# Keys and the first query pair of a windowed-attention trunk, seven block products for eight

## Chip, cores and metric

The kernel runs on one core of one Trainium2 chip. The metric is the device time of one execution in microseconds. Before the change three runs gave 1925.84, 1926.04 and 1926.89 us, so the median is 1926.04 us.

## What is computed

The reference is a trunk of two layers over 1024 tokens of width 1024, in float32. Layer 0 mixes tokens by a short gated convolution, layer 1 by attention in a window of 128 tokens; a SwiGLU of width 2816 follows each. Only the attention layer matters here:

```python
def swa_sink_attention(h, w_qkv, q_gain, k_gain, sinks, w_o):
    qkv = h @ w_qkv                       # 16 query heads, 4 key and 4 value heads of 64
    ...
    q = rmsnorm(q, q_gain)                # per head
    k = rmsnorm(k, k_gain)
    ...
    scores = jnp.einsum('bnqkgd,bnskd->bnkgqs', qb, kw).astype(jnp.float32) * scale
    ...                                   # ALiBi, window mask, a sink column, softmax
    out = jnp.einsum('bnkgqs,bnskd->bnqkgd', p.astype(vw.dtype), vw)
    return out.reshape(bsz, s, N_Q_HEADS * HEAD_DIM) @ w_o
```

## The kernel before

Everything lies transposed: features on the 128 partitions, the 1024 tokens along the free dimension, so the normed input `xs` is eight tiles of 128 features. To keep float32 accuracy every operand is split in a rounded part and a rest, and every block of a product is three matmuls of 128x512: rounded by rounded, rounded by rest, rest by rounded. A plain product of 128 output columns over all tokens is 8 x 3 x 2 = 48 such matmuls (`product`, L177).

Most products of the kernel are made another way, for a pair of 128 columns at once: the operands are cut in 2 x 2 blocks, and seven products of sums of blocks take the place of eight products of blocks. Each of the seven is four blocks of features deep and covers half of the tokens, 12 matmuls; a pair is 7 x 12 = 84 instead of 2 x 48 = 96. The weights of one of the seven are a granule of 128x512, loaded, rounded by one engine and its rest taken by another (`split_granule`). Products 0, 1 and 6 read blocks of `xs` itself; products 5, 2, 3 and 4 read sums of blocks (`operand_sums`, L1714), which are made once, stored to `q_ops` in HBM and loaded back for each pair. The sums of weight blocks are made beforehand by DMAs with addition (`added_sums`, L889, into `q_sums`).

The order of the work is written by hand. A `Line` (L842) holds TensorE work end to end, at 0.2265 us a matmul by its own count, and other instructions hung on it at times of that count; whatever stands earlier on the line is issued earlier, and each engine works through its instructions in that order. `attention_layer` (L1658) hangs keys and values on the line of layer 0 (`keys_and_values`, L1810): two plain products for the two key tiles, the values, one plain product for query tile 0. For a key tile `key_stats` (L1894) makes sums of squares by 16 matmuls of two columns, then on VectorE and ScalarE a mean, a logarithm, an exponential, a Newton step and a spread to 128x512; `key_rows` (L1920) transposes that spread, scales the keys, and writes the split keys `kz` (`part`: a ScalarE and a VectorE copy and two VectorE subtractions for each half of the heads). `keep_v` (L1771) brings the values out of PSUM.

After the line come steps (`step`, L2229). A step holds, in the order of the letters of `ORDER`, up to one unit of attention (the scores of one head tile and one block of 128 queries, the stages of earlier units) and three pieces of filling matmuls, five or six in all; `plan` and `agenda` put other instructions into steps. The scores of all units are written to one PSUM bank, `P0`, which `maxima` (L2079) on VectorE empties. `LAG` is the number of steps before the first unit. Before the change the filling is query tile 1 by a plain product (8 steps), then the query pairs 1 to 3 by sevens (`query_pairs`, L2285). `keep_q` (L1981) norms a query tile as keys are normed; its rests are taken on GpSimd (`part_lo`, L2029).

Of the kernel before, what the change touches and what calls it, by code (L numbers as in the profile page):

```python
# [15 lines left out]
P = 128  # L16
# [4 lines left out]
HD = 64  # L21
# [31 lines left out]
LAG = 12  # L53

QUERY_ORDER = (0, 5, 2, 6, 1, 3, 4)
STREAMED = (5, 2, 3, 4)
# [30 lines left out]
def trunk_kernel(ctx: ExitStack, tc: tile.TileContext, xT, small, w_in, w_out, w_qk, w_q, w_v, w_o, w_gu, w_dn, out):  # L87
# [746 lines left out]
    q_sums = tc.dram_tile((4, GROUP, P, 5 * P), F32, name="s4")  # L834
# [229 lines left out]
    def channel_mixer(layer, next_stage, src_of, operands, raw_tags, extra_tags, keep_tags, slots, begin_with=(), first_w=None, line=None, lead_in=None, before=None, follow=None):  # L1064
# [450 lines left out]
        def down_product(u, k, granules):  # L1515
# [24 lines left out]
            def square():  # L1540
                if first or k == 6:
                    sq = slot(f"s{h}" if first else f"G{8 + u % 2}", (P, HALF))
                else:
                    sq = slot("WL", (P, HALF), bufs=2)
# [40 lines left out]
        if layer == 0:  # L1585
            first_added_sums(1, line, begin + 10.0, 18.0)
            for u, n in ((1, 1), (2, 2)):
                dst = [q_sums[i, u : u + n][:, :, 0 : 4 * P] for i in range(4)]
                parts = [w_q[e, u : u + n][:, :, r] for e in (0, 1) for r in (0, 1)]
                added_sums(dst, parts, line, steady_begins + 75.0 * u - 45.0, 9.0)  # L1590
# [67 lines left out]
    def attention_layer():  # L1658
# [53 lines left out]
        v = []  # L1712

        def operand_sums(p, tags, t):  # L1714
# [6 lines left out]
            def first():  # L1721
                s["tiles"] = [slot(tag, (P, 2, 2, HALF), F32R) for tag in tags]
                s["t"] = [a[:, i] for a in s["tiles"] for i in (0, 1)]
                s["raw"] = [plain(x[:, 1]) for x in s["t"]]
                s["b12"] = plain(s["t"][3][:, 0])
# [17 lines left out]

            def store(i):
# [8 lines left out]
            for i in (0, 1):  # L1753
                at(t + 6.4, store, i)
# [55 lines left out]
        def keys_and_values():  # L1810
# [9 lines left out]
            def split(name, t, t_lo, hi_eng, lo_eng):  # L1820
                def hi():
                    w = it[name]
                    w.alloc()
                    act.copy(w.hi, w.raw) if hi_eng is act else hi_eng.tensor_copy(w.hi, w.raw)

                def lo():
                    w = it[name]
                    lo_eng.tensor_tensor(w.lo, w.raw, plain(w.hi), ALU.subtract)

                at(t, hi)  # L1830
                at(t_lo, lo)

# [765 lines left out]
```

## Time and profile before

| | |
|---|---|
| median of three runs | 1926.04 us |
| profiled execution, time and span | 1926.88 us, 1925.1 us |
| TensorE busy, share of the span | 1917.9 us, 100% |
| VectorE, ScalarE, GpSimd busy | 69%, 46%, 15% |
| mean granted clock of TensorE | 0.998 |

The profiled execution took 1.8 us beyond its span. In the profile PE is TensorE's matmuls, DVE is VectorE, ACT is ScalarE, POOL is GpSimd and SP the engine that issues most DMAs. A time behind a line (L170) is that of the kernel before. The ends of matmuls are modelled, so that neighbours overlap in the rows; the pace is read from one start to the next.

### The profile page before, as it was taken

To read this page: it belongs to the slowest core of one execution; us is meant where nothing else is said; L and a number is where in the kernel's file an instruction comes from. 1 tells how busy PE (TensorE), PEld (TensorE's weight loads), DVE (VectorE), ACT (ScalarE), POOL (GpSimd) and SP (SyncE) were. 2 spreads that over 40 slices of the span, in tenths; PEclk is the share of its full clock that TensorE was granted. 3 is DMA by queue.
4 is the path that set the end of the run, shared out by engine and by line. 5 is a ranking of instruction groups with operands and counts; after the bars stand their busy time and mean duration, and the time that the engine had idled before them with its cause. 6 is when DMAs were issued, how large, how long until landed. Compare 5 with 4: busy or idle time off the path is not lost.

```text
span 1925.1 us, 25387 instructions
## 1 busy us (share of the span) xinstructions
PE 1917.9 (100%) x9069; PEld 1604.1 (83%) x9069; DVE 1325.6 (69%) x2288; ACT 881.6 (46%) x1733; POOL 296.1 (15%) x382
## 2 busy tenths in 40 slices
PE   9999999999999999999999999999999999999999
PEld 8888888888888888888898888888888888888887
DVE  8997877975655666555775887788756665665543
ACT  5543464633333334544545787655233333344441
POOL 0011231011111100000023556310111111100000
PEclk9999999999999999999999999999999999999999
DMA  8897595377787638976255661142675575477562
GB/s 315 257 253 149 132 248 159 111 255 209 205 232 212 150 134 287 345 234 205 95 190 188 214 213 49 56 174 82 218 209 143 196 199 157 130 241 278 199 223 103
DMA packets 151262, 368.36 MB, mean 191 GB/s; under 512 B 15072, under 2 KB 26464, under 8 KB 151136
## 3 DMA queue, kind: packets, MB, share of 16 engines
q1 hardware_dynamic: 116864, 259.49, 39.5%
q0 software_dynamic: 34128, 107.23, 22.4%
q8 instruction: 71, 1.16, 0.2%
q14 instruction: 55, 0.45, 0.1%
q10 hardware_dynamic: 144, 0.03, 0.0%
HBM read 295.12 MB, written 145.23 MB: 229 GB/s over the span
## 4 chain that ended last, share of the span: by engine, by line
PE 96%; DVE 2%; ACT 1%; issue 1%; POOL 0%; POOLq 0%; DVEq 0%; ACTq 0%
PE acc L1002 16%; PE acc L1003 16%; PE acc L1005 16%; PE P L1002 10%; PE P L1003 10%; PE P L1005 10%; PE acc L170 4%; PE acc L2394 2%; PE acc L174 2%; PE P L2118 1%; PE acc L1132 1%; PE acc L1134 1%; PE acc L1133 1%; PE P L1676 1%; PE P L1793 1%; PE P L2075 1%
## 5 line engine op out<-in xcount | busy, mean ns | idle before, releaser
L1002 PE MATMUL acc<-XS,G 128*128 128x512 f32 x926 | 360.4, 389 | 0.0
L1003 PE MATMUL acc<-XS,G 128*128 128x512 f32 x926 | 360.2, 389 | 0.0
L1005 PE MATMUL acc<-XS,G 128*128 128x512 f32 x926 | 360.2, 389 | 0.0
L1002 PE MATMUL P<-A,G 128*128 128x512 f32 x550 | 214.1, 389 | 0.0
L1005 PE MATMUL P<-A,G 128*128 128x512 f32 x550 | 214.0, 389 | 0.0
L1003 PE MATMUL P<-A,G 128*128 128x512 f32 x550 | 214.0, 389 | 0.0
L1002 PEld LDWEIGHTS acc<-XS,G 128*128 128x128 f32 x926 | 173.8, 188 | 36.1
L1005 PEld LDWEIGHTS acc<-XS,G 128*128 128x128 f32 x926 | 173.8, 188 | 36.1
L1003 PEld LDWEIGHTS acc<-XS,G 128*128 128x128 f32 x926 | 173.8, 188 | 36.0
L1002 PE MATMUL acc<-A,G 128*128 128x512 f32 x442 | 172.1, 389 | 0.0
L1005 PE MATMUL acc<-A,G 128*128 128x512 f32 x442 | 172.0, 389 | 0.0
L1003 PE MATMUL acc<-A,G 128*128 128x512 f32 x442 | 171.9, 389 | 0.0
L936 DVE TENSOR_TENSOR G<-WL,G 128x512 fp32r<-128x512 f32 x168 | 115.1, 686 | 72.4 <-ACT G L935 72.4
L936 DVE TENSOR_TENSOR G<-WR,G 128x512 fp32r<-128x512 f32 (+1 forms) x216 | 144.4, 668 | 28.2 <-ACT G L935 28.2
L935 ACT CAST G<-WR 128x512 fp32r<-128x512 f32 (+1 forms) x216 | 130.5, 605 | 61.9 <-PE acc L1005 27.6
L935 ACT CAST G<-WH 128x512 fp32r<-128x512 f32 (+1 forms) x174 | 104.7, 602 | 84.3 <-PE acc L1005 41.1
L1334 ACT ACTIVATE G<-G 128x512 f32<-128x512 f32 x88 | 55.8, 634 | 159.6 <-DVE G L1431 152.4
L936 DVE TENSOR_TENSOR G<-WH,G 128x512 fp32r<-128x512 f32 (+1 forms) x174 | 115.7, 665 | 18.8 <-ACT G L935 18.7
L1005 PEld LDWEIGHTS P<-A,G 128*128 128x128 f32 x550 | 103.2, 188 | 21.4
L1003 PEld LDWEIGHTS P<-A,G 128*128 128x128 f32 x550 | 103.2, 188 | 21.4
L1002 PEld LDWEIGHTS P<-A,G 128*128 128x128 f32 x550 | 103.2, 188 | 21.4
L935 ACT CAST G<-WL 128x512 fp32r<-128x512 f32 x168 | 103.3, 615 | 24.5 <-DVE WL L884 12.9
(384 smaller groups left out, 3754.9 us busy)
## 6 DMA issues: line engine op xcount, KB each, us to landing
G<-h SPq DMA_DIRECT2D x70, 512.0 KB, 5.1
s<-in_w_dn SPq DMA_DIRECT2D x32, 704.0 KB, 7.7
h<-X POOLq DMA_DIRECT2D x44, 512.0 KB, 4.7
s<-s POOLq DMA_DIRECT2D x32, 704.0 KB, 7.3
WR<-s SPq DMA_DIRECT2D x74, 256.0 KB, 3.9
WR<-in_w_gu SPq DMA_DIRECT2D x36, 512.0 KB, 4.8
WH<-in_w_gu SPq DMA_DIRECT2D x36, 512.0 KB, 4.8
XS<-q_ops SPq DMA_DIRECT2D x36, 512.0 KB, 5.1
```

The costliest lines, as they stand in the source:

```text
L170: pe.matmul(ps.half(h), wh, xs[:, j, c], start=first and j == 0, stop=False)
L174: pe.matmul(ps.half(h), wl, xs[:, 0, c], start=False, stop=last)
L935: lambda: act.copy(out_hi, raw),
L936: lambda: lo_eng.tensor_tensor(out_lo, raw, plain(out_hi), ALU.subtract),
L1002: pe.matmul(ps, w[:, 0, c], x[:, 0, :], start=start and e == 0, stop=False, skip_group_check=True)
L1003: pe.matmul(ps, w[:, 0, c], x[:, 1, :], start=False, stop=False, skip_group_check=True)
L1005: pe.matmul(ps, w[:, 1, c], x[:, 0, :], start=False, stop=last, skip_group_check=True)
L1132: pe.matmul(ps, hi[:, kc], xs[:, 0, c], start=k == 0, stop=False, skip_group_check=True)
L1133: pe.matmul(ps, hi[:, kc], xs[:, 1, c], start=False, stop=False, skip_group_check=True)
L1134: pe.matmul(ps, lo[:, kc], xs[:, 0, c], start=False, stop=k == n_op - 1, skip_group_check=True)
L1334: state["silu"] = act.activation(x, x, AF.Silu)
L2394: pe.matmul(ps, g[:, w, c], x[:, b, :], start=begin and i == 0, stop=end and i == 2, skip_group_check=True)
```

## The change

The two key tiles become a pair of their own (`KEYS_AS_PAIR`) and query tiles 0 and 1 become pair 0; both go by sevens, on the line. The values are projected first. In these two pairs products 5, 2, 3 and 4 read the operand sums from the SBUF tiles in which they were made, and not from `q_ops`. The sums of squares of key tile 0 and 1 stand behind the sixth and the tenth of the 14 products, the transposes behind the 8th, 9th, 11th and 12th. The last of the values and of `kz` come in the first steps. `LAG` goes from 12 to 4. Operand sums use `G7` and `G4` for their raw sums and start earlier. Two more pairs of weights are summed by DMA, two weight tensors become one, and some tile names are swapped. The three pairs in the steps are as before.

```diff
-LAG = 12
+LAG = 4
...
+KEY_ORDER = (0, 1, 5, 2, 6, 3, 4)
+KEYS_AS_PAIR = 4
...
+                sq = slot(f"s{h}", (P, HALF)) if first else slot("WL", (P, HALF), bufs=2)
...
+            for i, (u, n) in enumerate(((0, 2), (2, 2), (KEYS_AS_PAIR, 1))):
+                dst = [q_sums[s, u : u + n][:, :, 0 : 4 * P] for s in range(4)]
                 parts = [w_q[e, u : u + n][:, :, r] for e in (0, 1) for r in (0, 1)]
...
+                if not workspace:
+                    rooms_ = [slot(tag) for tag in ("G7", "G4")]
+                    workspace.extend(a[:, h] for a in rooms_ for h in (lo_half, hi_half))
+                s["raw"] = [workspace[i] for i in (1, 2, 3, 0)]
+                s["b12"] = workspace[0]
...
-            load(("k", 0), w_qk[NK], NK, t - 12.0)
-            load(("k", 1), w_qk[NK + 1], NK, t - 9.0)
-            split(("k", 0), t - 5.5, t - 4.4, act, dve)
-            split(("k", 1), t + 2.2, t + 3.4, act, dve)
             for q in (0, 1):
-                load(("wv", q), w_v[:, 4 * q : 4 * q + 4, :], 4, t + (-2.5, 4.7)[q])
-                at(t + (7.0, 13.5)[q], split_v, q)
-                load(("q", q), w_qk[q], NK, t + 15.5 + q)
-                split(("q", q), t + (28.0, 44.0)[q], t + (29.0, 45.0)[q], dve, pool)
-            operand_sums(0, ("A2", "A3"), t - 1.0)
-            operand_sums(1, ("A0", "A1"), t + 5.5)
-            operand_sums(2, ("A4", "A5"), t + 13.0)
-            operand_sums(3, ("A2", "A3"), t + 19.5)
-            at(t + 16.0, score_buffers)
-
-            def project(name):
-                it[name, "acc"] = Acc()
-                yield from product(it[name, "acc"], it[name], xs)
-
-            def project_work(name):
-                steps = project(name)
-                for _ in range(3 * NK):
...
+            def part(g, e, i):
+                if g not in kz:
+                    kz[g] = pair_slot(f"A{g}"), pair_slot(f"A{g + 2}")
+                hi, lo = kz[g]
+                raw = key_raw[g]
+                rows, rest = (slice(x * HD, (x + 1) * HD) for x in (e, 1 - e))
+                if i == 0:
+                    act.copy(hi[rows, e, :], raw[rows, :])
+                elif i == 1:
+                    dve.tensor_copy(hi[rest, e, :], raw[rows, :])
+                else:
+                    to = rows if i == 2 else rest
+                    dve.tensor_tensor(lo[to, e, :], raw[rows, :], plain(hi[rows, e, :]), ALU.subtract)
...
+            project_values(0)
             line.work(4, mean)
             at(line.end + 0.05, token_rows)
-            project_keys(1)
-            key_stats(0)
-            project_values(0)
-            key_rows(0)
-            key_stats(1)
             project_values(1)
-            key_rows(1)
-            project_work(("q", 0))
+            operand_sums(3, ("G8", "G10", "G9", "G11"), line.end + 0.1)
+            first_pairs()
...
+        seq = [(KEYS_AS_PAIR, k) for k in KEY_ORDER] + [(u, k) for u in range(NK // 2) for k in QUERY_ORDER]
+        n_first = 2 * KINDS
...
+            rooms["raws"] = [x[:, i] for x in (wr, g0, g1) for i in (0, 1)]
+            rooms["grans"] = wl + [rooms["spare"], slot("G2", (P, 2, 4 * P), F32R)]
+            rooms["banks"] = [bank(f"P{i}") for i in range(3)]
...
+        def split_granule(j, hi_eng=dve, lo_eng=pool):
+            g, raw = gran_room(j), raw_room(j)
+            act.copy(g[:, 0], raw) if hi_eng is act else hi_eng.tensor_copy(g[:, 0], raw)
+            lo_eng.tensor_tensor(g[:, 1], raw, plain(g[:, 0]), ALU.subtract)
+
+        def bank_of(u, k):
+            four = rooms["banks"]
+            return four[2] if k in (4, 5, 6) else four[(u + 1) % 2 if k != 1 else u % 2]
...
+        def part_of_x(k, p):
+            return xs[2 * p + (k != 0)][:, :, halves_of[k == 6]]
...
+            def stats(g):
+                s["st", g] = bank("P3")
+                head_stats(s["st", g], s["side", g], 0, NB)
...
+            def wide(g, q):
+                spread(act, s["side", g][:, halves_of[q]], s["y", g][:, 4 * q : 4 * q + 4, :])
+
+            def rows(g, q):
+                s["rows"] = bank("P3")
+                turn_blocks(s["rows"], s["side", g][:, halves_of[q]])
+
+            def scale(g, q):
+                raw = key_raw[g][:, halves_of[q]]
+                dve.scalar_tensor_tensor(raw, raw, qkg, s["rows"], ALU.mult, ALU.mult)
...
+            def of_product(j, p):
+                u, k = seq[j]
+                x = summed[p][STREAMED.index(k)] if k in STREAMED else part_of_x(k, p)
+                all_of(three(j, p, x))
+
+            def stats_work(g):
+                line.work(4, stats, g)
+                t = line.end
+                at(t + 0.1, log, g)
+                at(t + 0.9, guess, g)
+                at(t + 1.6, newton, g)
+                for q in (0, 1):
+                    at(t + 2.4 + 0.6 * q, wide, g, q)
+
+            def rows_work(g, q):
+                line.work(2, rows, g, q)
+                at(line.end + 0.05, scale, g, q)
...
+            for j in range(n_first):
+                begins[j] = line.end
+                u, k = seq[j]
+                for p in range(NK // 2):
+                    line.work(3, of_product, j, p)
+                t = line.end
+                finish(u, k, lambda f, t=t: at(t + 0.05, f))
+                if j in (4, 6):
+                    g = 0 if j == 4 else 1
+                    for h in (0, 1):
+                        at(t + 0.8 + 0.65 * h, squares, g, h)
+                if j in (5, 9):
+                    stats_work(0 if j == 5 else 1)
+                if j in (7, 8, 10, 11):
+                    rows_work(j // 10, (j - 7) % 3)
+                if j == 9:
+                    for i in range(4):
+                        at(t + 0.1 + 0.5 * i, keep_v, 0, i)
+                    for e in (0, 1):
+                        for i, d in enumerate((2.1, 2.1, 3.3, 4.6)):
+                            at(t + d + 3.3 * e, it["part"], 0, e, i)
+                if j == 11:
+                    s["base"] = t
+            for j in range(n_first + 2):
+                if j < n_first:
+                    t = begins[j - 3] + 0.05 if j > 3 else begin + 14.0 + 2.4 * j
+                    at(t, split_granule, j, act, dve)
+                if j < 6:
+                    at(begin + 2.0 + 1.2 * j, load_granule, j)
+                else:
+                    at(begins[j - (6 if j < n_first else 4)] + 0.02, load_granule, j)
+            at(begins[n_first - 1] + 0.05, split_granule, n_first, act, dve)
+            for n in range(4):
+                at(begins[4] + 3.0 * n, load_operand, n)
+            at(begins[11] + 0.1, load_operand, 4)
+            at(begins[13] + 0.1, score_buffers)
+            pos["free"] = "P3"
...
+            def planned_from(d, f):
+                t = s["base"] + 1.3 * d
+                if t < line.end - 0.2:
+                    at(t, f)
+                else:
+                    agenda.setdefault(max(round((t - line.end) / 0.65) / 2, 0), []).append(f)
+
+            keep_q(0, lambda: raw_of_even(0), plan_=planned_from)
...
+                plan(0, lambda j=j: split_granule(j + 1, dve, dve if j < n_first + 2 else pool))
+                load_granule(j + 2)
...
-            keep_q(0, it[("q", 0), "acc"])
-            w = it["q", 1]
-            pairs = query_pairs()
-            for j in (0, 1):
-                pairs.load_granule(j)
-            pairs.load_operand(4)
-            for n in (5, 6):
-                pairs.load_operand(n)
-            acc = Acc()
-            work = product(acc, w, xs)
-            for k in range(NK):
-                step(work)
-                if k % 2:
-                    pairs.load_operand(k // 2)
-                if k == 5:
-                    pairs.split_granule(0)
-            run(work)
-            pairs.load_operand(7)
-            keep_q(1, acc, pairs.odd_raw)
...
+            rooms["banks"] = [bank("acc") for _ in range(4)]
+            pos["values"] = rooms["banks"][3]
+            for n in (5, 6, 7):
+                load_operand(n)
+            for i in range(4):
+                plan(0.5 * i, lambda i=i: keep_v(1, i))
+            for e in (0, 1):
+                for i, d in enumerate((1.0, 1.0, 2.0, 3.0)):
+                    plan(d + 2 * e, lambda e=e, i=i: it["part"](1, e, i))
+            keep_q(1, lambda: rooms["odd"], later=4)
```

## Rows read from the trace of the kernel before

**Rows 1.** The page: busy time of each engine; the chain that ended last.
```profile
PE 1917.9 (100%) x9069; PEld 1604.1 (83%) x9069; DVE 1325.6 (69%) x2288; ACT 881.6 (46%) x1733; POOL 296.1 (15%) x382
...
PE 96%; DVE 2%; ACT 1%; issue 1%; POOL 0%; POOLq 0%; DVEq 0%; ACTq 0%
```

**Rows 2.** PE's waits, whole span: us in total, times, longest.
```profile
PE P L2075 <- DVE mx L2090: 1.2, 3, 0.5
```

**Rows 3.** Windows: length, busy of PE, PEld, DVE, ACT, POOL, clock, DMA share, GB/s.
```profile
1014.00:1025.00 11.00, 11.00 (x61) 9.33 (x60) 2.08 (x8) 2.88 (x7) 1.17 (x2) 1.00 0.73 262
1025.00:1034.00 9.00, 9.00 (x52) 7.79 (x50) 4.49 (x7) 4.74 (x10) 5.73 (x4) 1.00 0.72 253
1034.00:1060.00 26.00, 26.00 (x161) 22.66 (x160) 20.01 (x66) 19.23 (x60) 11.68 (x10) 0.93 0.52 167
```

**Rows 4.** Timeline of PE: start, length, line, tiles, count, idle before.
```profile
951.05 1.07 PE L170 MATMUL acc<-XS,WH 128*128 128x512 f32 x4
...
961.93 1.84 PE L1884 MATMUL P<-cst,s 128*128 128x1 f32 x16
...
974.66 1.84 PE L1676 MATMUL acc<-cst,G 128*128 128x2 f32 x16
976.36 0.37 PE L1766 MATMUL acc<-G,XS 128*128 128x256 f32 x1
...
1023.03 0.60 PE L1793 MATMUL P<-cst,G 128*128 128x128 f32 x4
1023.39 0.70 PE L170 MATMUL acc<-XS,WH 128*128 128x512 f32 x2
...
1051.98 0.36 PE L2075 MATMUL P<-A,G 128*128 128x192 f32 x1
```

**Rows 5.** Timeline of ACT around the values and key tile 1.
```profile
983.81 0.47 ACT L1779 ACTIVATE A<-acc,r 128x256 fp32r<-128x256 f32 x1 [0.55 <-DVE A L1780]
...
990.93 0.22 ACT L1695 ACTIVATE hr_y<-hr_m 128x16 f32<-128x16 f32 x1 [1.26 <-DVE hr_m L1683]
...
992.86 1.14 ACT L1788 COPY G<-hr_y 128x512 f32<-128x512 f32 x2 [0.66 <-DVE hr_y L1709]
994.02 1.05 ACT L1942 CAST A<-G 64x1024 fp32r<-64x1024 f32 x1
```

**Rows 6.** Timeline of DVE, from the end of layer 0 into the steps.
```profile
951.25 0.69 DVE L1532 TENSOR_TENSOR X<-X,acc 128x512 f32<-128x512 f32 x1 [2.59 <-PE acc L1005]
...
983.29 0.48 DVE L1780 SCALAR_TENSOR_TENSOR A<-acc,r,A 128x256 fp32r<-128x256 f32 x1 [0.97 <-ACT A L1779]
...
992.65 0.18 DVE L1709 SCALAR_TENSOR_TENSOR hr_y<-hr_t,hr_y 128x16 f32<-128x16 f32 x1
...
995.20 0.69 DVE L1944 CAST A<-G 64x1024 fp32r<-64x1024 f32 x1
995.90 2.46 DVE L1947 TENSOR_TENSOR A<-G,A 64x1024 fp32r<-64x1024 f32 x2
...
1027.84 0.43 DVE L2338 CAST WL<-WR 128x512 fp32r<-128x512 f32 x1 [1.59 <-PE acc L174]
1028.30 1.66 DVE L2340 TENSOR_TENSOR WL<-WR,WL 128x512 fp32r<-128x512 f32 x1
...
1032.66 0.69 DVE L2340 TENSOR_TENSOR WL<-WR,WL 128x512 fp32r<-128x512 f32 x1
...
1051.04 0.48 DVE L2090 CUSTOM_DVE_ANT_0 s<-P,cst 128x192 f32<-128x192 f32 x1
```

**Rows 7.** Timeline of POOL: the rests of query tile 0.
```profile
1025.16 5.96 POOL L2032 TENSOR_TENSOR G<-G,G 64x512 fp32r<-64x512 f32 x4 [1.76 <-ACT G L2027]
```

**Rows 8.** Windows, PE alone: length, PE busy, clock, DMA share, GB/s.
```profile
1034.50:1035.00 0.50, 0.50 (x4) 0.76 0.87 336
...
1038.00:1038.50 0.50, 0.50 (x5) 0.83 0.93 254
```

**Rows 9.** DMA issues: tiles, queue, count, KB each, median us to landing.
```profile
WR<-s SPq DMA_DIRECT2D x74, 256.0 KB, 3.9
```

More of the change, by code (lines that the diff above doesn't have):

```diff
@@ new lines, in part_of_x, with three @@
+        def part_of_x(k, p):
+            return xs[2 * p + (k != 0)][:, :, halves_of[k == 6]]
+        def three(j, p, x):
+            u, k = seq[j]
+            ps, g = bank_of(u, k), gran_room(j)
+            c = slice(p * P, (p + 1) * P)
+            begin, end = k in (0, 1, 4, 5) and p == 0, p == NK // 2 - 1
+            for i, (w, b) in enumerate(((0, 0), (0, 1), (1, 0))):
+                pe.matmul(ps, g[:, w, c], x[:, b, :], start=begin and i == 0, stop=end and i == 2, skip_group_check=True)
+                yield
@@ new lines, in attention_layer, with room, load_operand @@
+        loads = [(k, p) for u, k in seq[n_first:] if k in STREAMED for p in range(NK // 2)]
+        first_rooms = {}
+        used = {"n": 0}
+        def room(n):
+            if n >= 5 and n < 8:
+                if n not in first_rooms:
+                    first_rooms[n] = slot(("G10", "G11", "G9")[n - 5], (P, 2, HALF), F32R)
+                return first_rooms[n]
+            r = n if n < 5 else (n - 8) % 5
+            return xs[2 * r][:, :, hi_half] if r < 4 else rooms["spare"]
+        def load_operand(n):
+            if n < len(loads):
+                k, p = loads[n]
+                src = q_ops[p, STREAMED.index(k)].rearrange("p (j c) -> p j c", c=HALF)
+                nc.sync.dma_start(plain(room(n)), src)
@@ new lines, in after_use, with work_of_pairs @@
+        def after_use(n):
+            if n < 5:
+                load_operand(n + 8)
+            elif n >= 8:
+                load_operand(n + 5)
+        def work_of_pairs():
+            n = 0
+            for j in range(n_first, len(seq)):
+                u, k = seq[j]
+                plan(0, lambda j=j: split_granule(j + 1, dve, dve if j < n_first + 2 else pool))
+                load_granule(j + 2)
+                for p in range(NK // 2):
+                    streamed = k in STREAMED
+                    x = room(used["n"]) if streamed else part_of_x(k, p)
+                    steps = three(j, p, x)
+                    for i in range(3):
+                        next(steps)
+                        n += 1
+                        if i == 2 and streamed:
+                            after_use(used["n"])
+                            used["n"] += 1
+                        if i == 2 and p == NK // 2 - 1:
+                            finish(u, k, soon)
+                            if k == 1:
+                                keep_q(2 * u, lambda u=u: raw_of_even(u))
+                            if k == 4:
+                                raw, side = raw_of_odd(u)
+                                keep_q(2 * u + 1, lambda raw=raw: raw, side, later=3 if u + 1 < NK // 2 else 2)
+                        if n % 7 in (2, 4, 5, 0):
+                            yield
```

348 lines of the change are left out of this document (121 added, 227 removed).

## Prediction

> **What bounds the kernel now.** The page comes first: TensorE is busy all of the span and 96% of the chain that ended last is TensorE's [rows 1]. So two things can move the time: how many matmuls there are, and whether TensorE has to wait. The waits of TensorE come next: in the steps it waits for VectorE three times, 1.2 us in all, each time for the maxima that empty the one bank of scores [rows 2]; between 951 us, where the attention layer begins, and 1075 us no wait of it is listed. The windows say what the other engines do there: in the 20 us ahead of the first scores VectorE works 2.08 + 4.49 = 6.6 us, and in the next 26 us, with attention, 20.0 us [rows 3]. So VectorE enters the steps rested and has some 6 us to spare in the first of them. The timeline of TensorE gives the prices: 48 matmuls of 128x512 from 951.05 to 961.93, 0.2267 us each; a burst of 16 matmuls of two columns from 974.66 to 976.36, 1.70 us, where the line counts 4 x 0.2265 = 0.91; four transposes from 1023.03 to 1023.39, 0.36 us [rows 4]. A thing to see there is how close VectorE already is: the maxima of a unit start at 1051.04 and take two instructions of 0.48 us, and the next unit's scores start at 1051.98, just behind them [rows 4, 6].
>
> **The matmuls.** Two pairs of 96 matmuls become two of 84. 24 x 0.2267 = 5.44 us less. Bursts, transposes and values stay in number. This term is certain.
>
> **The first wait: key tile 1.** Take the end of product 10 as zero. TensorE does the burst for key tile 1 (1.70) and product 11 (12 x 0.2267 = 2.72), and at 4.42 it comes to the transposes of the spread of key tile 1, which are work of the line itself: all 3 products left stand behind them. Between burst and spread lie one VectorE mean, a logarithm, an exponential, three small VectorE instructions and a ScalarE spread. By themselves they would take 0.2 + 0.22 + 0.22 + 3 x 0.18 + 0.57, under 2 us [rows 5, 6], ready at 3.7. But the change hangs the values of the first half and key tile 0 on the line at the same place, and they are issued ahead. ScalarE has, in order: the copy of product 10's bank (0.57 as the spread's half), two values (0.47 each), a granule (0.57), the logarithm, two values, the exponential, a part of key tile 0 (1.05) and then the spread: from 0.2 to 5.3 without a single pause. And it pauses: the second value of a bank waits until VectorE has read the first, 0.55 us in the row at 983.81 [rows 5], and VectorE has its own queue: value rests 0.48 each, the granule's rest 0.69, a cast of key tile 0 of 0.69, all ahead of steps of the chain [rows 6]. Going down both queues:
>
> ScalarE bank copy to 0.8, value to 1.2; VectorE rest to 1.7; ScalarE value to 2.2, VectorE rest to 2.7; ScalarE granule to 2.8, VectorE its rest to 3.5; mean 3.6, logarithm 3.9; ScalarE value to 4.2, VectorE rest to 4.8, value to 5.3, exponential to 5.4; VectorE rest and cast to 6.5, ScalarE key part to 6.4; VectorE's last two small ones to 6.8; spread to 7.4.
>
> TensorE waits from 4.42 to about 7.45, 3.0 us. Bounds: 0 if the chain were issued first, 0.9 by ScalarE's own work alone, 4 if each hand-over costs 0.1 us more. I take 3.0, since every one of these instructions has a row.
>
> **The second wait: the first steps.** Take the end of product 14 as zero. Ahead of the first scores are now 4 steps, 21 matmuls (4.76 us) and two groups of transposes (0.72). Before there were 12 steps, some 20 us, in which VectorE was two thirds idle [rows 3]. The second unit's scores come 5 matmuls later; with the first unit's own (0.4, an estimate from the four transposes) TensorE is there at 7.0. They need the first unit's maxima, and ahead of these VectorE has in its queue: product 14's bank 0.69; two scalings of query tile 0, 1.38; four rests of values, 1.92; two granules, 2 x (0.43 + 0.69) = 2.24; of key tile 1 two casts, 1.38, and two subtractions, 2.46; the maxima, 0.96 [rows 6]. That is 11.0 us, some 10 with neighbours overlapping by 0.07, from 0.3 on: done at 10.3 at best. It also pauses, for the transposes, which come at 1.1 and 2.9, and for values that ScalarE rounds only behind the parts of query tile 0. Going down the queues again I come to 12.0. So TensorE loses 12.0 - 7.0 = 5.0 by the second unit, in pieces: at granules 16 and 17 whose rests are in the same queue (0.5 and 1.5), at the first scores, since GpSimd's first two rests of query tile 0 (1.3 to 1.5 each [rows 7]) end at 6.9 (0.7), at the first transposes (0.3), at the second scores (2.0). The last two subtractions of key tile 1 (2.46) fall in the next two steps and cost 1.4 more over the units that follow. Sum 6.4. Bounds: 3.1 if VectorE never pauses and takes all of the last two in its stride; 0 if it kept up; 9 with hand-overs 0.1 us longer. I take 6.4, nothing in the rows lying between VectorE's work and the scores.
>
> **The clock.** The granted clock falls twice in the attention layer. The first fall, 1034.6 to 1038.1, stands at 0.50 [rows 8], the lower level of 1.2 GHz, and costs half of 3.4, 1.7 us; a burst of two-column matmuls and the short first scores lie just ahead of it. After the change a burst is followed 2.7 us later by a wait of 3 us, and I count a fall there, +1.7. The fall at the first scores I leave, but among waits, where a slower TensorE costs about half: -0.85. Net +0.85; bounds -1.7 (no fall in either place) and +3.4.
>
> **What costs nothing.** Granules are loaded six products ahead, over 16 us, and land in 3.9 [rows 9]; their rooms are free from the first microseconds of the layer. Values first: the two splits of the value weights (each 0.69 + 1.23) and the earlier operand sums go into the 10 us ahead of the layer, where VectorE sat idle 2.59 us in front of its last addition alone [rows 6]; a key split of 1.23 goes from there. If that cover were gone, the first values would start up to 2 us late. Operand sums 3 are made beside products 1 and 2 and read first by product 3's last block, some 8 us after their start, against 4.5 us of work. Reading sums from SBUF spares TensorE nothing. The DMA sums of two more pairs of weights, the squares in another tile, and the swapped names lie in stretches where TensorE does not wait at all [rows 2].
>
> **Sum.** -5.44 + 3.0 + 6.4 + 0.85 = +4.8. On the profiled execution, 1925.1 of span and 1.8 around it, 1926.88 us, that is 1931.7. This execution is 0.84 above the median, so against the median of 1926.04 I predict 1930.9.
>
> **A rule that would make it worse.** A rest that VectorE took from two SBUF tiles lasted 1.66 us at 1028.30, while GpSimd was at its rests of query tile 0 (1025.16 to 1031.1); the same instruction took 0.69 at 1032.66 with GpSimd idle [rows 6, 7]. The Trainium skill, "SBUF — State Buffer", section "SBUF: two separate sides", says that VectorE with two SBUF inputs and GpSimd contend for one pair of ports, and that whichever comes first keeps it for its whole instruction. The trace agrees with that rule in this one place. As a mechanism of this kernel, from the rows alone: the change puts five such VectorE instructions (granule rests, subtractions of key tile 1) beside four such rests of GpSimd in the first steps, and at 1.66 - 0.69 = 0.97 us each that is 4.9 us more in VectorE's queue: 1930.9 + 4.9 = 1935.8.
>
> **The rivals.** (a) No waits: faster. If the spread of key tile 1 is ready within 4.42 us of product 10's end, and key tile 1's parts are through VectorE before the second unit, only the matmuls count: 1926.04 - 5.44 = 1920.6, and 1918.9 if the fall at 1034.6 goes too. For it speaks that no wait is listed in this stretch now; against it that ScalarE's queue alone ends at 5.3. It decides itself at that spread. (b) One of the two waits, or both at their lower bounds with the clock as before: -5.44 + 3.0 is 1923.6, -5.44 + 6.4 is 1927.0, -5.44 + 0.9 + 3.1 is 1924.6: no change that can be told. (c) The port above: 1935.8.
>
> **How the numbers follow.** A measurement of this kernel can tell about 0.2%, 3.9 us: faster is below 1922.2, slower above 1929.9. Both waits about as sized: 0.53, of which 0.41 slower and 0.12 within 0.2%, since the sum is only 1 us past that bound. (a) 0.16, faster. (b) 0.21, same. (c) 0.10, slower. So 0.16 faster, 0.33 same, 0.51 slower. The range goes from the case without waits, 1920.6, to just short of the port's, 1935.5; the likeliest case's own is 1928 to 1934.
>
> **What would show it.** In the profile after: 24 matmuls less; a wait of TensorE of about 3 us some 59 us behind the layer's start at the transposes of key tile 1, released by ScalarE's spread; the second scores some 5 us late, released by the maxima, with VectorE busy without a break for 10 us ahead of them; the waits for the maxima in the list going from 1.2 us to 4 or more. It is wrong if the spread comes in time, if VectorE is idle ahead of the first maxima, or if the clock falls elsewhere.

## The result, and the profile after

The changed kernel takes 1934.05 us (median of 6 runs, 1931.52 to 1935.99); the kernel before, six runs too, 1925.41 us (1924.46 to 1926.89). The ratio is 1.0044, 95% interval 1.0031 to 1.0057: slower by 0.44%, 8.6 us between the medians, and 3.1 us above the 1930.9 that was predicted. The profiled execution took 1933.8 us with a span of 1932.0, 6.9 more than the span before. Those 6.9 are what the two traces can explain. They are less than 8.6, because the profiled execution of the kernel before took 1926.88 us, 1.5 above its median. The page of the changed kernel, against [rows 1]: 24 matmuls less, and a chain of TensorE's that lost four points to VectorE, ScalarE and a DMA.

```profile
PE 1914.6 (99%) x9045; PEld 1596.9 (83%) x9045; DVE 1337.5 (69%) x2305; ACT 887.6 (46%) x1746; POOL 295.2 (15%) x386
...
PE 92%; DVE 3%; ACT 2%; issue 1%; DMA 1%; POOL 0%; SPq 0%; ACTq 0%; DVEq 0%; POOLq 0%
```

TensorE's listed waits in the attention layer were 1.4 us, 1.2 of them for maxima [rows 2], from 1078 us on; now they sum to 11.1 us (L328 lies outside the layer). The old waits for maxima are still there, 1.1 us. The timeline gives the five new ones a place, 9.66 us together. The top of the list:

```profile
PE P L2185 <- DVE mx L2200: 3.4, 4, 2.2
PE acc L1991 <- issue: 3.1, 1, 3.1
PE P L1804 <- ACT G L1799: 2.9, 1, 2.9
PE P L328 <- DVE s L325: 1.5, 1, 1.5
PE P L2185 <- POOL G L2145: 0.8, 1, 0.8
```

TensorE's timeline of the changed kernel, the instructions that waited:

```profile
1013.60 0.66 PE L1804 MATMUL P<-cst,G 128*128 128x128 f32 x4 [2.90 <-ACT G L1799]
1026.49 0.66 PE L1804 MATMUL P<-cst,G 128*128 128x128 f32 x4 [0.57 <-POOL G L1799]
1032.11 0.30 PE L2185 MATMUL P<-A,G 128*128 128x64 f32 x1 [0.83 <-POOL G L2145]
1036.65 1.19 PE L1991 MATMUL acc<-WH,WL 128*128 128x512 f32 x2 [3.13 <-issue]
1040.06 0.53 PE L2185 MATMUL P<-A,G 128*128 128x192 f32 x1 [2.23 <-DVE mx L2200]
```

Read from above, TensorE waited at the transposes of key tile 1's spread (called key tile 1's rows from here on, after `rows_work`), at those of query tile 0, at the first unit's scores, at granule 16 (counted from 0) and at the second unit's scores. The line of granule 16 names no releaser, but VectorE's lines below give one: the granule's cast ends at 1036.55, and the matmul starts at 1036.65. These are the lines of VectorE and GpSimd ahead of the first maxima:

```profile
1027.19 0.69 DVE L1809 TENSOR_TENSOR G<-G,P 128x512 f32<-128x512 f32 x1 [0.93 <-PE P L1804]
...
1030.97 1.63 DVE L1871 CAST A<-G 64x1024 fp32r<-64x1024 f32 x1
...
1033.04 2.10 DVE L1874 TENSOR_TENSOR A<-G,A 64x1024 fp32r<-64x1024 f32 x1
1035.07 1.48 DVE L1934 CAST WL<-WR 128x512 fp32r<-128x512 f32 x1
1036.65 0.69 DVE L1935 TENSOR_TENSOR WL<-WR,WL 128x512 fp32r<-128x512 f32 x1
...
1039.32 0.34 DVE L2200 CUSTOM_DVE_ANT_0 s<-P,cst 128x64 f32<-128x64 f32 x1
```
```profile
1029.42 2.64 POOL L2145 TENSOR_TENSOR G<-G,G 64x512 fp32r<-64x512 f32 x2 [2.43 <-DVE WL L1935]
1032.79 3.47 POOL L2145 TENSOR_TENSOR G<-G,G 64x512 fp32r<-64x512 f32 x2 [0.73 <-ACT G L2140]
```

VectorE is busy from 1027.19 to the end of the first maxima, about 1039.9, with no listed pause. Three instructions that take 0.69, 1.22 and 0.43 elsewhere take 1.63, 2.10 and 1.48 here, each beside a rest of GpSimd: 2.87 us more. The windows, the first three over the same times as in [rows 3]:

```profile
1014.00:1025.00 11.00, 11.00 (x61) 9.37 (x60) 8.40 (x12) 4.17 (x9) 0.43 (x4) 1.00 0.01 2
1025.00:1034.00 9.00, 7.11 (x36) 5.00 (x34) 7.76 (x15) 5.63 (x10) 4.93 (x5) 1.00 0.75 252
1034.00:1060.00 26.00, 21.01 (x125) 17.90 (x126) 22.60 (x56) 14.23 (x46) 8.60 (x9) 0.87 0.33 109
1036.00:1037.00 1.00, 0.35 (x1) 0.39 (x2) 0.90 (x2) 0.00 (x0) 0.26 (x1) 0.73 1.02 395
1037.00:1043.00 6.00, 3.77 (x11) 2.67 (x11) 5.83 (x14) 2.20 (x9) 1.05 (x1) 0.50 0.38 118
```

VectorE's load in the 20 us ahead of 1034 went from 6.6 to 16.2 us. In the layer the granted clock is at the lower level, 1.2 GHz, once, from about 1036.5 to 1043.3. The fall begins in the wait for granule 16; TensorE worked some 4.4 us at that level, so it cost 2.2.

Landmarks say where the time goes. The pairs end 3.0 us earlier (1024.62 for 1027.59). The ninth unit's scores come 6.6 us later (1061.24 for 1054.61), and the distance is 7.0 from 1085 to 1158. So nearly all of the loss is there eight units into attention. Later the two traces differ twice more, and this about cancels. The clock of the kernel before falls a second time at 1178, which costs it 1.7. The changed kernel has no such fall, but it loses 0.5 at 1190 (a wait of 0.33 and what the modelled ends hide) and 1.5 from 1265 to 1280, in short gaps of the matmuls behind the last units; these were not traced further.

### The profile page after: what moved, and what is told of

It reads as the page before. It is cut to its first block, busy times and chain, and to the rows that moved or that the text cites. A ratio compares the mean times of both kernels' runs of the same rounds, so it can differ in the third digit from the quotient of the medians.

```text
span 1932.0 us, 25403 instructions
## 1 busy us (share of the span) xinstructions
PE 1914.6 (99%) x9045; PEld 1596.9 (83%) x9045; DVE 1337.5 (69%) x2305; ACT 887.6 (46%) x1746; POOL 295.2 (15%) x386
## 4 chain that ended last, share of the span: by engine, by line
PE 92%; DVE 3%; ACT 2%; issue 1%; DMA 1%; POOL 0%; SPq 0%; ACTq 0%; DVEq 0%; POOLq 0%
PE acc L1004 16%; PE acc L1007 16%; PE acc L1005 16%; PE P L1004 10%; PE P L1005 10%; PE P L1007 10%; PE acc L172 2%; PE acc L1991 2%; PE P L1991 2%; PE P L2228 1%; PE acc L176 1%; PE P L1675 1%; PE P L2185 1%; DMA WR<-in_w_o 1%; PE P L1804 1%
## 5 line engine op out<-in xcount | busy, mean ns | idle before, releaser
L901 POOL DMA_DIRECT2D s<-s x68 | 60.0, 893 | 357.5 <-DMA s<-s 176.6
```

The costliest lines, as they stand in the source:

```text
L901: nc.gpsimd.dma_start(dst[to], dst[of], accum_op=ALU.add)
```

## Experiments

The first theory was that the order of work in ScalarE's and VectorE's queues makes two separate waits, so that each goes when the work in front of it is moved. The rivals were that the clock makes the loss by itself, that the port that VectorE and GpSimd share is the root, or that VectorE has too much to do in this stretch, whatever the order. Ratios are to the kernel before; the changed kernel's is 1.0044 (1.0031 to 1.0057). The runs were made on several chips, so versions are compared by these ratios and not by their times. The interval of every version but the last overlaps with the changed kernel's: for them the ratio says only that little was won or lost, and what an edit did is read from its trace. Behind a product means after it in TensorE's order.

**Key tile 1's rows one product later.**

```diff
-                if j in (7, 8, 10, 11):
-                    rows_work(j // 10, (j - 7) % 3)
+                if j in (7, 8, 11, 12):
+                    rows_work(j // 11, (j - 7) % 4)
...
-                    s["base"] = t
+                    s["base"] = t + 0.5
```

> The transposes of key tile 1 stand one product later (behind products 12 and 13 of the 14, for 11 and 12); query tile 0's chain begins 0.5 us later. If the first wait comes from ScalarE's queue order alone (the spread was ready 2.9 us after TensorE got there, a product takes 2.7 us): the 2.90 us wait falls to at most 0.3, the other new waits stay (6.8 us together) and the span falls by 2.4 to 2.9, to about 1929.3. If the time won here only meets the later waits (the queue of VectorE in the first steps is anchored elsewhere): those waits grow by as much and the span stays within 0.5 of 1932.

1938.12 us, ratio 1.0065 (1.0051 to 1.0079): no faster, and by its median slower still. The wait went, as the first line shows, and came back in two pieces at the next instructions:

```profile
1013.76 0.66 PE L1804 MATMUL P<-cst,G 128*128 128x128 f32 x4 [0.18 <-ACT G L1799]
1019.56 0.63 PE L1804 MATMUL P<-cst,G 128*128 128x128 f32 x4 [2.39 <-DVE G L2030]
1022.19 3.54 PE L1675 MATMUL P<-cst,G 128*128 128x2 f32 x16 [1.31 <-DVE G L2030]
...
1025.00:1030.00 5.00, 5.00 (x14) 4.05 (x15) 0.96 (x6) 0.91 (x3) 1.17 (x2) 0.50 0.00 0
```

Both wait for the scalings of key tile 1, which stand behind key tile 0's parts on VectorE. And the clock fell behind the first of them and stayed at 0.50 from 1020.8 to 1031: the burst took 3.54 us for 1.84. The last line is of the windows. The waits at the first scores, granule 16 and the second scores stayed as they were (0.85, 3.14, 2.23).

**The values and key tile 0's parts 4 us later.**

```diff
-                        at(t + 0.1 + 0.5 * i, keep_v, 0, i)
+                        at(t + 4.1 + 0.5 * i, keep_v, 0, i)
...
-                        for i, d in enumerate((2.1, 2.1, 3.3, 4.6)):
+                        for i, d in enumerate((6.1, 6.1, 7.3, 8.6)):
```

> The transposes stay where they are; instead the eight reads of the first half of the values and key tile 0's parts are planned 4 us later, so that key tile 1's logarithm, exponent and spread are ahead of them in ScalarE's and VectorE's queues. If the order of these queues is the cause: the 2.90 us wait falls to under 0.5, the span falls by about 2.5 to 2.9, as in the other way of taking the wait away. If the wait comes from the statistics themselves (two-column matmuls, logarithm, exponent, Newton step): it stays above 2 and the span does not move.

1933.10 us, 1.0040 (1.0027 to 1.0053). The 2.90 us wait is off the list, so order was its cause. 2.80 us came back at query tile 0's rows, with a fall of the clock behind it (1025.9 to 1029.3):

```profile
1025.58 0.84 PE L1804 MATMUL P<-cst,G 128*128 128x128 f32 x4 [2.80 <-POOL G L1799]
```

**Key tile 1's parts four steps later.**

```diff
-                    plan(d + 2 * e, lambda e=e, i=i: it["part"](1, e, i))
+                    plan(d + 4 + 2 * e, lambda e=e, i=i: it["part"](1, e, i))
```

> Key tile 1's eight part instructions (four on VectorE 5.6 us of its queue ahead of the second unit's maxima, two on ScalarE ahead of them, the rest behind) are planned four steps later. If VectorE's queue makes the second group of waits: the three waits at the first two scores and at granule 16 (0.83 + 3.13 + 2.23 = 6.2 us) fall to under 2, the stretch at half clock behind them shortens, and the span falls by 4 to 6, to 1926 to 1928. If the clock alone makes the loss: the fall at 1035 to 1045 stays and with it most of the 6.9 us. If the moved work only waits elsewhere: new waits of 2 us or more for maxima in steps 4 to 10 and a span within 1.5 of 1932.

1931.83 us, 1.0032 (1.0019 to 1.0045). The waits for granule 16 and the second scores went, 5.4 us, so VectorE's queue made them. At the sixth unit's scores 2.63 us of wait for the maxima came back, and the clock fell there, 0.62 on the mean from 1045 to 1054:

```profile
1046.95 0.53 PE L2185 MATMUL P<-A,G 128*128 128x192 f32 x1 [2.63 <-DVE mx L2200]
```

So the last case of the expectation, work that only waits elsewhere, held for the larger part.

**Query tile 0's rests on VectorE.**

```diff
-                pool.tensor_tensor(q[rest, :, e, :], ...
+                (dve if i == 0 else pool).tensor_tensor(q[rest, :, e, :], ...
```

> Query tile 0's four rests (GpSimd, 64x1024 each in two halves, 6.1 us of GpSimd in all) are made on VectorE, so that GpSimd touches SBUF no longer while VectorE works its queue ahead of the first maxima. VectorE's queue gets about four times 0.69 us longer (2.8) and loses the stretched instructions (1.63, 2.10, 1.48 back to 0.69, 1.22, 0.43: 2.9 us less, 3.4 with the later one). If the queue's content is the cause and the shared port only lengthens it: the first maxima come within 0.7 us of where they were and the span stays within 1 of 1932. If the port is the root: the waits at the first scores shrink by 3 us or more and the span falls to 1929 or under.

1933.31 us, 1.0038 (1.0025 to 1.0050). The lines that answer to the stretched ones above:

```profile
1032.28 0.69 DVE L1871 CAST A<-G 64x1024 fp32r<-64x1024 f32 x1
...
1034.80 1.22 DVE L1874 TENSOR_TENSOR A<-G,A 64x1024 fp32r<-64x1024 f32 x1
1035.94 0.41 DVE L1934 CAST WL<-WR 128x512 fp32r<-128x512 f32 x1
```

All are at their usual length, so GpSimd stretched them. The time hardly moved, since the rests now stand in VectorE's queue themselves: the first scores wait 2.31 us for them, for 0.83, and the second scores come at 1040.48, for 1040.06. In this execution the clock also fell behind the first wait, which put query tile 0's rows 1.3 us later. So GpSimd lengthens VectorE's queue, but it is not the root of the waits.

**Waits filled with matmuls.** 12 matmuls into an unused bank where TensorE waits for granule 16, 9 where it waits for the second scores.

```diff
+        def fill(n):
...
+            for _ in range(n):
+                pe.matmul(pos["values"], q, kz[0][0][:, 0, 0:HALF], start=True, stop=True)
```

> The changed kernel with 21 more matmuls of 512 columns into a bank that is free (12 in the wait at granule 16, 2.7 us of 3.13; 9 in the wait at the second scores, 2.0 of 2.23): TensorE works on where it rested, nothing else differs. Price of the clock: from 1040 to 1043.2 3.1 us of matmuls ran at half the clock, so a clock that does not fall saves 1.6 us here, span 1930.4. If the clock is the cause of the waits too (it falls, work is late, buffers come late): the waits shrink and the span falls by 4 or more. If the fall doesn't hang on the rest: no change, or up to 0.5 more.

1934.29 us, 1.0044 (1.0030 to 1.0058). The fall at 1036 went: from 1034 to 1045 the mean clock is 1.00. Its 2.2 us were not won. The waits for maxima in the list went only from 3.4 us to 2.8, although 2.04 of them were now filled: 0.64 is left at 1041.33, and two new ones of 0.40 and 0.62 come at 1043.84 and 1046.55.

```profile
1041.33 0.36 PE L2192 MATMUL P<-A,G 128*128 128x192 f32 x1 [0.64 <-DVE mx L2207]
```

With TensorE at full clock, VectorE was late. So the clock does not make the loss by itself. The other executions say the same: the five here have a mean granted clock of 0.998 to 1.000, the six of the changed kernel 0.996 to 0.998, and the ratio is the same. The profiled execution also shows a fall from 1013.6 to 1017.0 behind the first wait, some 1.7 us, which that of the changed kernel does not.

**VectorE's work on GpSimd.** There are four versions. The first has key tile 1's parts four steps later, with their rests on GpSimd. The second has the values later, key tile 0's rests on GpSimd and query tile 0's spread on ScalarE. The third is the second with key tile 1's parts later. The fourth has all eight rests on GpSimd, and of key tile 1 the casts on ScalarE, the parts four steps later, and the rows behind product 12 and in the middle of product 13. The line that moves the rests, with `g == 0` in the second and third and no condition in the fourth:

```diff
-                    dve.tensor_tensor(lo[to, e, :], raw[rows, :], plain(hi[rows, e, :]), ALU.subtract)
+                    (pool if g == 1 else dve).tensor_tensor(lo[to, e, :], ...
```

> Key tile 1's parts four steps later, as before, and its four rests (1.22 us each on VectorE) on GpSimd. With the parts only moved, 3.79 us of waits for maxima came back at 1047 (2.63 in one), because VectorE was full there too. If the amount of VectorE's work is the cause: that wait falls under 1, the fall of the clock behind it goes, and the span falls by another 3 to 4 from 1930.7, to 1927. If GpSimd's port use costs VectorE as much as it takes off, or the granules' rests queue behind the new ones on GpSimd: waits for WL rests or for maxima of 2 us or more, and 1930 to 1933.

> First half of the values and key tile 0's parts 4 us later (which alone only moved the 2.9 us to query tile 0's rows, 2.8 us, with a fall of the clock behind it), and now key tile 0's four rests on GpSimd and query tile 0's spread on ScalarE, so that VectorE has 4.9 us less from 1012 to 1024. If VectorE's amount of work there was what came back: neither the 2.9 nor the 2.8 us wait remains (under 0.7 together), no fall of the clock before 1030, and the span falls by 4 to 5 from 1931.3, to 1926 to 1927, with the waits at the first scores as they were. If they only move on to the first scores, these grow by as much and the span stays within 1 of 1931.

> The edits of the run before (values later, key tile 0's rests on GpSimd, query tile 0's spread on ScalarE) together with key tile 1's parts four steps later on VectorE. If the two stretches are lost to one thing, VectorE's amount of work from 1007 to 1045, and each edit takes its own stretch: about 1931.3 - 4.5 - 1.5 = 1925, of which the later waits for maxima (3.8 us) are what is left over the 1920.6 without waits. If the edits only push one lump of work along: 1930 or more.

> VectorE loses 9.8 us of rests (all eight of the key tiles' parts on GpSimd) and the two casts of key tile 1 (on ScalarE); key tile 1's parts are four steps later; key tile 1's two groups of transposes stand behind product 12 and in the middle of product 13. If the loss is the amount of VectorE's work from 1007 to 1048, first as waits of 2 us or more and then as half clock behind each: no wait over 1 us is left before the tenth unit, no fall of the clock before 1100, the ninth unit's scores come at 1050 to 1052 (before: 1054.6, changed kernel: 1061.2) and the span is 1921 to 1923. If the waits only move on (GpSimd's rests now late for the first scores or for a granule, VectorE's casts stretched beside them): a wait of 2 us or more with a fall behind it at one of these, and 1927 to 1931.

In this order 1930.59 us, 1.0030 (1.0018 to 1.0041); 1934.44, 1.0050 (1.0037 to 1.0063); 1932.78, 1.0040 (1.0028 to 1.0053); 1933.40, 1.0036 (1.0022 to 1.0049). Taking 5 to 11 us off VectorE gained 2.7 us at best, by the ratios 1.0030 and 1.0044. The last one shows why, in VectorE's and GpSimd's lines behind product 10; TensorE then waited 4.43 us, until 1018.24, for the spread:

```profile
1012.86 2.23 DVE L1707 SCALAR_TENSOR_TENSOR hr_t<-hr_t,hr_m 128x16 f32<-128x16 f32 x1
1015.12 2.36 DVE L1708 SCALAR_TENSOR_TENSOR hr_y<-hr_t,hr_y 128x16 f32<-128x16 f32 x1
```
```profile
1012.64 4.81 POOL L1874 TENSOR_TENSOR A<-G,A 64x1024 fp32r<-64x1024 f32 x2 [26.08 <-ACT A L1869]
```

In the changed kernel these two take 0.17 us each:

```profile
1012.46 0.17 DVE L1707 SCALAR_TENSOR_TENSOR hr_t<-hr_t,hr_m 128x16 f32<-128x16 f32 x1
1012.67 0.17 DVE L1708 SCALAR_TENSOR_TENSOR hr_y<-hr_t,hr_y 128x16 f32<-128x16 f32 x1
```

The first ends at 1015.09, with GpSimd's first rest (4.81 / 2, to 1015.05); the second at 1017.48, with its second (1017.45). The Trainium skill, "SBUF — State Buffer", section "SBUF: two separate sides", says that a VectorE instruction with two SBUF inputs and a GpSimd instruction lock each other out of one pair of ports, and that the one that comes first keeps it for its whole length. The lines agree to 0.04 us. They show what this makes of a chain of small instructions, here the Newton step that key tile 1's spread needs. The version with key tile 0's rests on GpSimd has the same at 1022.78, 2.36 us for a small instruction and 3.8 us of wait behind it.

**Order alone, and order with key tile 1.** Behind product 10: half of key tile 0's parts in a gap of VectorE's, then key tile 1's chain, then the values. The second version adds key tile 1's parts later, rests on GpSimd.

```diff
+                        at(t + 4.1 + 0.5 * i, keep_v, 0, i)
+                    for e, ds in enumerate(((0.1, 0.1, 2.6, 2.9), (5.5, 6.0, 7.3, 11.5))):
...
+                for i, d in enumerate((3.0, 3.5, 4.0, 4.5)):
+                    plan(d + 1.5 * e, lambda e=e, i=i: it["part"](1, e, i))
```

> The same instructions on the same engines as the changed kernel, in another order on ScalarE and VectorE behind product 10: first the first half of key tile 0's parts (its casts in the gap that VectorE had at 1004.4 to 1007, its rests behind key tile 1's Newton step), then key tile 1's spread, then the reads of the first half of the values, and the last rest behind query tile 0's Newton step. If order alone makes the first wait and moved it to query tile 0's rows when the values went later: both waits (2.90 and 0.57 in the changed kernel, 2.80 in the run with the values later) come to 1 us or less together, no clock fall before 1030, the first scores at 1029.2 to 1030.5, span 1929 to 1930. If the sum of VectorE's work sets it, whatever the order: a wait of 2 us or more again before the first scores, and the span within 1 of 1932.

> That order, and in the first steps key tile 1's parts two to three steps later with their four rests on GpSimd. If the two stretches are separate: 1929.5 less the 2.6 to 3.5 that the same step with GpSimd gave by itself, so 1926 to 1927, the kernel before's time. If VectorE's small instructions wait for GpSimd's long ones, as at 1012.86 and 1015.12 where two of 0.17 us took 2.23 and 2.36 beside rests of 2.4 us: more, with such instructions in VectorE's rows at 1035 to 1050 and waits for maxima of 2 us or more.

1933.02 us, 1.0040 (1.0028 to 1.0053), and 1932.48 us, 1.0031 (1.0020 to 1.0043). With order alone the rows' waits fell from 3.47 to 1.74 us and the first scores came 1.7 us earlier. The waits behind them stayed, and the clock was then at the lower level for 10.2 us (from 1032.9) where it had been for 6.8. In the second the fifth unit's scores came at 1044.35, level with the kernel before (1044.16), although the clock had fallen at 1021.1. Then TensorE waited 3.23 us, until 1050.26, for the maxima. VectorE and GpSimd just ahead of it:

```profile
1045.70 2.24 DVE L1703 TENSOR_TENSOR hr_y<-hr_y,cst 128x16 f32<-128x16 f32 x1
1047.87 0.16 DVE L1707 SCALAR_TENSOR_TENSOR hr_t<-hr_t,hr_m 128x16 f32<-128x16 f32 x1
1048.07 1.22 DVE L1708 SCALAR_TENSOR_TENSOR hr_y<-hr_t,hr_y 128x16 f32<-128x16 f32 x1
```
```profile
1040.41 7.50 POOL L1874 TENSOR_TENSOR A<-G,A 64x1024 fp32r<-64x1024 f32 x3
1047.99 1.26 POOL L1935 TENSOR_TENSOR WL<-WR,WL 128x512 fp32r<-128x512 f32 x1
```

Query tile 1's Newton step waits for the third rest (to 1047.91) and again for a granule's (to 1049.25), and the maxima stand behind it in the queue.

**GpSimd's rests clear of the Newton step.** This is the second of those two versions with key tile 1's casts on ScalarE and its rests at other places.

```diff
-                    dve.tensor_copy(hi[rest, e, :], raw[rows, :])
+                    (dve.tensor_copy if g == 0 else act.copy)(hi[rest, e, :], raw[rows, :])
...
+                for i, d in enumerate(((3.0, 6.0, 4.5, 5.0), (4.5, 9.0, 8.0, 9.0))[e]):
+                    plan(d, lambda e=e, i=i: it["part"](1, e, i))
```

> The same order behind product 10 as in the two runs before; key tile 1's two casts on ScalarE instead of VectorE; its four rests on GpSimd, placed so that two lie ahead of query tile 1's Newton step and two behind it, none beside its instructions of 0.17 us. If those instructions waited for GpSimd's rests (2.24 and 1.22 us in the run before, and the wait of 3.23 us for the maxima behind them): each is back at 0.16 to 0.18, the wait of 3.23 falls under 0.6 and the fall of the clock behind it goes (another 1.7), the casts stretched beside GpSimd (1.07 and 1.96) are off VectorE; the ninth unit's scores come at 1053 to 1055 for 1060.6, span 1923 to 1926, that is within 1.5 of the kernel before on either side. If those instructions waited for something else (the logarithm on ScalarE): they stay long, a wait of 2 us or more stays at the sixth unit, and the span is 1929 or more.

1928.69 us (11 runs, 1926.30 to 1930.95), ratio 1.0012 (1.0003 to 1.0021): by the ratios 6 us faster than the changed kernel, clear of its interval, and still 0.1% slower than the one before. The longest waits of the layer, a line of the Newton step and the windows:

```profile
PE P L2185 <- DVE mx L2200: 1.9, 5, 0.4
PE P L1804 <- POOL G L1799: 1.5, 1, 1.5
...
PE P L2185 <- POOL G L2145: 0.8, 1, 0.8
```
```profile
1043.40 0.17 DVE L1703 TENSOR_TENSOR hr_y<-hr_y,cst 128x16 f32<-128x16 f32 x1
```
```profile
1036.00:1039.00 3.00, 2.80 (x24) 2.42 (x22) 1.30 (x2) 2.95 (x7) 2.92 (x2) 1.00 0.96 376
1039.00:1046.00 7.00, 6.70 (x27) 5.44 (x27) 5.59 (x17) 3.16 (x13) 4.38 (x4) 0.56 0.14 46
```

The small instructions are back at 0.16 to 0.18, and no wait for maxima is over 0.44. Waits of 1.53 and 0.83 us are left, at query tile 0's rows and at the first scores. The clock still fell, from 1039.9 to 1046.7, behind query tile 1's burst and not behind a long wait; TensorE worked 6.5 us at that level, so it took 3.3 of the 5.44 that the matmuls gave. No version here beats the kernel before. Two were not tried: the old order of values and keys with the new products, and a larger `LAG`, which would put more filling matmuls ahead of the first scores.

## Why the prediction was right

**Matmuls.** There are 24 less, 9045 for 9069. The pairs end 3.0 us earlier: 5.44, less the first wait, and 0.7 for query tile 0's two groups of transposes, which now stand behind the pairs. This term was right.

**The first wait.** 3.0 was predicted and 2.90 measured, at key tile 1's rows, from 59.5 to 62.4 us behind the layer's start, released by ScalarE's spread. The working holds step by step, not only in its sum: from the end of product 10 the exponential ends at 5.2 us, for 5.4, and VectorE's last small instruction at 6.9, for 6.8. That order is its cause is shown: with the values behind the chain it fell to nothing, or 0.2.

**The second wait.** By the second unit's scores 5.0 was predicted, with 1.4 to follow; 6.76 was measured (0.57 + 0.83 + 3.13 + 2.23). The place and the releaser were right, and VectorE was full for 12.7 us with the instructions that the prediction lists, all but product 14's bank. The working was less good than its sum. It had the first maxima done 12.0 us behind product 14, and they were done at 15.3. VectorE did not pause between its instructions; it started them late, with the first scaling at 1027.19, 2.6 us behind product 14. And the sum left out GpSimd's 2.87 us, most of the 3.3 that were missing, which stood in the prediction as a separate rival at one in ten and 4.9 us. That rival was part of the mechanism; with GpSimd's rests moved to VectorE, the time saved was about what the rests then cost. The 1.4 to follow came as no listed wait. One sign missed its size: the list's waits for the maxima went to 3.4 us, not to 4 or more, because the longest piece was granule 16's 3.13, where 2.0 had been given to granules 16 and 17 together.

**The clock.** This term was off. It put a fall of 1.7 behind the first wait. Five profiled executions have this wait behind the same instructions; that of the changed kernel and that with key tile 1's parts later show no fall, the other three show one (key tile 1's rests on GpSimd, query tile 0's on VectorE, filled waits). So it is a chance, not a term. It may also be part of what spreads the changed kernel's runs over 4.5 us: the three at a mean granted clock of 0.998 took 1931.5 to 1933.8 us, and the three at 0.996 or 0.997 took 1934.3 to 1936.0. The fall at the first scores was to stay half hidden; it became longer, 2.2 us of cost for 1.7. The second fall of before, at 1178, which cost 1.7, did not recur.

**The sum.** +4.8 was predicted for the profiled execution and +6.9 measured; between the medians it was +4.9 and +8.6. To the ninth unit the terms found are 0.1 (a later start) - 5.44 + 9.66 + 2.2 - 1.7 = 4.8, of 6.6 us. Of the other 1.8, 0.8 are in the five waits themselves: a listed wait begins at the modelled end of the matmul before it. Read from that matmul's start to the next, less its own pace (0.2267 us, or twice that at the lower clock), they are 3.06, 0.74, 0.99, 3.30 and 2.40, 10.5 together. Two short gaps, ahead of 1052.25 and 1061.24, are 0.5 more; the last 0.5 was not traced. So the direction and the two waits were foreseen, but that the time lies in the stated range owes something to the range, whose upper end came from the port's case. 1934.05 is just past the 1928 to 1934 of the case that came.

**Rivals.** That no wait comes is out, by the list. That only one comes is out too. What none of them said is what the experiments showed: the two waits are not two. VectorE has work for 43.2 of the 51.2 us from 1010 to the ninth unit, against 24.1 of 44.6 before (the changed kernel's window first):

```profile
1010.00:1061.20 51.20, 41.39 (x231) 33.60 (x229) 43.21 (x93) 27.75 (x72) 15.15 (x17) 0.93 0.36 118
1010.00:1054.60 44.60, 44.60 (x250) 38.26 (x249) 24.06 (x69) 22.47 (x62) 17.29 (x15) 0.96 0.55 189
```

Of these 19.1 us more, 15.4 are work that lay ahead of 1010 or just across it before ([rows 6] show its first pieces from 983.29 on) and lies behind it now: 8 rests of the key tiles at 1.22, 4 casts at 0.69, 6 value rests at 0.48. Stretched instructions make 3.4 us, against 1.0 before. With the values projected last, that work had the projection of the values beside it; projected first, they are through TensorE before it can begin, and the rooms for their reads are held by operand sums until products 10 and 14. That reading is from the rows and the code and was argued, not shown, as the old order with the new products was not tried. Shown is that moving one piece of the work moved the wait, and that order, casts on ScalarE and rests on GpSimd outside the small chains together left no wait over 1.53 us. Whether fewer of these would do was not tried.

## What to carry to other kernels

When a block product removes matmuls, add up what the other engines do in the same stretch before placing anything: with VectorE at a load of 84%, as here, a wait taken away came back at the next instruction that needed VectorE. Before handing work to GpSimd, look which small two-input instructions of VectorE lie beside it; a chain of 0.17 us steps next to 2.4 us rests cost a rest for each step that came beside one. And price a wait as long as those here with the half clock that can follow it, as a chance, since behind the same wait of 2.9 us it came in three executions of five.

## What was not expected of the hardware

VectorE's casts with a single SBUF input were held up beside GpSimd's rests as well as instructions with two: 0.43 became 1.48 and 0.69 became 1.63 us in the changed kernel, and 2.37 us in the last version, where a cast begun at 1038.12 ended at 1040.49, 0.27 us behind GpSimd's rest. GpSimd was held up in turn: two rests took 3.47 us for 2.64 beside VectorE's longest. The clock fell at 1039.9 in the last version with no listed wait of TensorE over 0.9 us in the 14 us ahead of it, 0.6 us after the end of a burst of two-column matmuls (1037.58 to 1039.28). It fell at 1021.1 in the version with order and key tile 1 too, 0.5 us after such a burst, with no listed wait over 0.4 us in the 11 us ahead. Other bursts, as at 1046.73 in the changed kernel, were followed by full speed.
